# Dilated attention by residue classes instead of masked full steps, with the squares' sums of the attention tail on the tensor engine

## The chip, the cores and the metric

One Trainium2 chip (trn2), all 8 cores. The batch of 16 sequences is split over the cores, two sequences each, and every core runs the same program on its own two, one after the other. The time is the device time of the slowest core in microseconds (us). TensorE is called PE below, VectorE DVE, ScalarE ACT, GpSimd POOL, SyncE SP; PSUM is the memory that PE writes its results to. The form of a matmul is the size of its stationary tile, rows*columns (128*128, 64*128 or 128*64); where two matmuls in a row have different forms, that is a change of form.

Some executions of any kernel here fall into a slower state, in which the cores of one die (or of both) show a lower granted TensorE clock: one such run of the changed kernel had 0.85 to 0.86 on die 1 and 0.99 on die 0, and took 3242.6 us. Such runs are marked slow and are left out of all comparisons.

## The reference

A decoder layer: half a SwiGLU feed-forward network (FFN), a mixer, and another half FFN, each between two RMS norms. The mixer has 4 differential heads and 8 dilated heads of 64 columns. What matters here are the dilated heads:

```python
DIL_PATTERNS = ((128, 1), (512, 4), (2048, 16))   # (window, dilation)

def dilated_pattern(q, k, v, slopes, window, dil):
    """query t attends t, t-d, t-2d, ..., t-window."""
    ...
    bias = -slopes[:, None, None] * (dsub * dil)       # true token distance
    s = jnp.where(valid, s * D ** -0.5 + bias, -inf)
    ...                                                # softmax: o, lse
    return o, lse

def dilated_attention(q, k, v, slopes):
    ...                                                # the three patterns
    w = jax.nn.softmax(jnp.stack(lses, axis=0), axis=0)
    return sum(w[i][..., None] * outs[i] for i in range(3))

def hybrid_mixer(h, ...):
    ...
    return jnp.concatenate([o_d, o_l], axis=-1) @ w_out
```

Weighting the three softmaxes by their own denominators is one softmax in which a key counts once for every pattern that holds it. With count(d) = [d <= 128] + [d % 4 == 0 and d <= 512] + [d % 16 == 0 and d <= 2048], the weight of a key at distance d is count(d) * exp(score - slope * d). Both kernels compute that. At distances from 129 to 512 three keys in four have the count 0, beyond 512 fifteen in sixteen.

## The kernel before

The program is written by a scheduler in the host code: it keeps a model of when each engine will be free, and picks at each point a score step (S), a value step (A) or a piece of other work (F: a projection matmul, a transpose), so that PE has something to do while exponentials and multiplies are under way. Heads are handled in 8 units: units 0 to 3 are one differential head each (with two score maps), units 4 to 7 two dilated heads each. While unit u runs, the projections of unit u+1 are its filler; the last unit's filler is the output projection.

A step of a unit covers 512 queries and 128 keys, for both heads (or maps); `...` marks what is cut here and below:

```python
steps = [(Q, kt) for Q in range(NTT) for kt in range(4 * Q + 4)]       # 40 steps a unit
...
def do_scores(Q, kt, ji):
    mp = kt - 4 * Q
    c0 = max(mp, 0) * 128
    ...
    for m in range(2):                                                 # one head in each 64 rows of PE
        S.op(PE, lambda e, m=m: e.matmul(
            sp[:, m, c0:TT], KT[i][64 * m:64 * m + 64, kt * 128:(kt + 1) * 128],
            QT[i][64 * m:64 * m + 64, Q * TT + c0:(Q + 1) * TT], start=True, stop=True), ...)
    ...
            S.op(ACT, lambda e, ...: e.activation(o_, i_, AF.Exp, bias=bias, scale=SCALE), ...)
    ...
        lazy.append((bm, cost, lambda: S.op(DVE, lambda e: e.tensor_tensor(   # dilated: x count mask (bf16)
            P[:, :, c0:TT], P[:, :, c0:TT],
            masks[:, m0 + c0:m0 + TT].unsqueeze(1).broadcast_to([128, 2, TT - c0]), ALU.mult), ...)))

def do_av(Q, kt, ji):
    for m in range(2):
        for uq in uqs:                                                 # 128 queries each
            S.op(PE, lambda e, ...: e.matmul(
                a_ap, P[:, m, uq * 128:(uq + 1) * 128], Vt[i][:, kt, vc:vc + w1], ...))   # w1 = 65
```

The 65th column of the values is ones, so that the denominator comes out beside the output. The output has queries in the partitions; a reciprocal and a multiply close it, and four transposes on PE bring it into the form that the output projection reads.

The sum of squares for the norm after the output projection is kept by POOL, 512 columns at a time, and PE adds over the partitions once at the end:

```python
class Stat:
    def add(self, si):
        ...
            S.op(POOL, lambda e: e.tensor_tensor(dst[:], sacc[k][:], sq[si][:], ALU.add), ...)
    def finish(self, k2):
        S.op(PE, lambda e: e.matmul(bank(pb), ones_bf[:], ssum[k][:], start=True, stop=True), ...)
        return rstd(pb, k2, ...)
```

The softmax here doesn't subtract the row's maximum and nothing guards it: scores larger than these inputs give would overflow.

Of the kernel before, what the change touches and what calls it, by code (L numbers as in the profile page):

```python
# [23 lines left out]
TT = 512  # L24
# [6 lines left out]
MOFF, MLEN = 384, 1536  # L31
# [197 lines left out]
def _dil_count(d):  # L229
    c = np.zeros_like(d, dtype=np.float32)  # L230
    c += ((d >= 0) & (d <= 128))
    c += ((d >= 0) & (d % 4 == 0) & (d <= 512))
    c += ((d >= 0) & (d % 16 == 0) & (d <= 2048))
    return c


def _consts():
    masks = _dil_count(np.arange(-MOFF, MLEN - MOFF)[None, :] - np.arange(128)[:, None])
# [6 lines left out]
    return masks, tri, btab, ident  # L245


def build_program():
# [10 lines left out]
    masks_d = dt_in("c_masks", [128, MLEN])  # L259
# [3 lines left out]
    outT_d = nc.dram_tensor("outT", [NSEQ, D, SEQ], F32, kind="ExternalOutput").ap()  # L263
    wdb_d = [nc.dram_tensor("wdb%d" % i, [NKC, 128, NF * 128], BF16, kind="Internal").ap() for i in range(2)]

    with ExitStack() as st:
# [5 lines left out]
        U_B = 79936  # L272
# [3 lines left out]
        masks = sb("masks", [128, MLEN], BF16)  # L276
# [6 lines left out]
        lamv = sb("lamv", [128, 256], F32)  # L283
# [7 lines left out]
        sg = [sb("sg%d" % i, [128, TT], F32) for i in range(2)]  # L291
# [25 lines left out]
        QT, KT, Vt, B_QT, B_KT, B_V, B_V1 = [], [], [], [], [], [], []  # L317
# [15 lines left out]
        assert off <= o_y + 16384  # L333
        off = o_y + 16384
        o_tail = off
        o0, B_o0 = [], []
        for i in range(2):
            o = carve(2048)
            o0.append(U[:, o // 2:o // 2 + 1024].bitcast(F32).rearrange("p (a c) -> p a c", a=4))
            B_o0.append([RU.buf("o0_%d_%d" % (i, a), o + a * 512, o + a * 512 + 512) for a in range(4)])  # L340
        NP = 5
# [6 lines left out]
        o = carve(2048)  # L348
        osq = U[:, o // 2:o // 2 + 1024].bitcast(F32).rearrange("p (a c) -> p a c", a=4)
        B_osq = RU.buf("osq", o, o + 2048)  # L350
        Otok, B_Otok = [], []
        for i in range(2):
            o = carve(1024)
            Otok.append(U[:, o // 2:o // 2 + 512].rearrange("p (a c) -> p a c", a=4))
            B_Otok.append([RU.buf("Otok%d_%d" % (i, a), o + a * 256, o + a * 256 + 256) for a in range(4)])
        assert off <= U_B, (off, U_B)
# [26 lines left out]
        def y_mix(d):  # L383
            return xn[:, d, 2 * TT:4 * TT].bitcast(F32), B_yo[d]

        y_free = [U[:, o // 2:o // 2 + TT * 2].bitcast(F32)
                  for o in [NKC * SEQ * 2 + k * 2048 for k in range(6)] + [o_y + 12352]] + [sg[0][:]]
        B_ya = [RU.buf("ya%d" % k, o, o + 2048)
                for k, o in enumerate([NKC * SEQ * 2 + k * 2048 for k in range(6)] + [o_y + 12352])]
        B_sg = [Buf("sg%d" % i) for i in range(2)]  # L390
        B_ya.append(B_sg[0])
# [6 lines left out]
        B_lam = Buf("lam")  # L398
# [4 lines left out]
        B_sml = [[Buf("sml%d_%d" % (i, j)) for j in range(5)] for i in range(3)]  # L403
        B_wdb = [[Buf("wdb%d_%d" % (i, d)) for d in range(NKC)] for i in range(2)]
# [41 lines left out]
        def late_consts():  # L446
# [7 lines left out]
            S.op(DVE, lambda e: e.reduce_sum(lamt[:, 0:1], lamv[:, 0:64], AX.X), reads=[B_lam], writes=[B_lam])  # L454
            S.op(DVE, lambda e: e.reduce_sum(lamt[:, 1:2], lamv[:, 128:192], AX.X), reads=[B_lam], writes=[B_lam])
            S.op(ACT, lambda e: e.activation(lamt[:, 2:4], lamt[:, 0:2], AF.Exp), reads=[B_lam], writes=[B_lam])
            S.op(DVE, lambda e: e.scalar_tensor_tensor(lamt[:, 4:5], lamt[:, 3:4], -LAM_INIT, lamt[:, 2:3],
                                                       ALU.add, ALU.subtract),
                 reads=[B_lam], writes=[B_lam])
            S.dma(POOL, ident[:], ident_d, writes=[B_cpool], kb=32)  # L460
            S.dma(POOL, tri[:], tri_d, writes=[B_cpool], kb=32)
            S.dma(POOL, masks[:], masks_d, writes=[B_cpool], kb=384)
# [6 lines left out]
        class Stat:  # L469
# [19 lines left out]

            def finish(self, k2):  # L490
# [4 lines left out]

        stat_banks = [6, 7]
# [15 lines left out]
        def prenorm_items(tt, gcol, tag):  # L512
            state = {}

            def p_sq(kc):
                def fn():
                    if kc == 0:
                        assert not pre_active
                        pre_active.append(1)
                        state["st"] = Stat(0)  # L520
# [806 lines left out]
```

## Time and profile before

Five runs before the prediction: median 2996.79 us, from 2992.37 to 3129.73 (the longest is a slow run). I cut the attention of each sequence into four stages by what PE does, with one rule for every kernel, so a few borders differ by up to 3 us from those in the prediction. "Steady" begins with the first matmul of a dilated form (in the kernel before that is a 65-column value product, and 8 dilated score matmuls already stand in the 5 us ahead of it) and ends with the first matmul of the output projection; "mixed" ends with the last value or denominator product; "tail" ends where the second FFN begins (16 FFN matmuls that run early in the kernel before, from 1036.7 us, are counted back at the full rate).

| stage, us of the slowest core (before) | sequence 0 | sequence 1 | what PE has in it |
|---|---|---|---|
| differential | 261.8 | 263.0 | differential heads, projections as filler |
| steady | 167.2 | 167.8 | dilated heads, projections as filler |
| mixed | 75.9 | 74.2 | rest of the last dilated unit, output projection as filler |
| tail | 44.2 | 42.7 | rest of the output projection, norms |
| sum | 549.1 | 547.7 | |

How to read it: the change touches the last three rows, 287 us of sequence 0 and 285 of sequence 1. The rest of the 2990.8 us of the profiled core is the differential stage and the FFNs. The cores differ in one place: the tail of sequence 0 lasts about 45 us on cores 1 and 6 (the slowest) and about 35 on the six others, for a reason that I did not look into.

### The profile page before, as it was taken

How to read it: one execution, taken by the hardware profiler on the slowest of the kernel's cores; microseconds unless marked ns; L12 is line 12 of the kernel's file. 1: busy time of each engine (PE TensorE's matmuls, PEld its weight loads, DVE VectorE, ACT ScalarE, POOL GpSimd, SP SyncE). 2: the span in 40 equal slices, each digit the busy share in tenths (PEclk: the TensorE clock that was granted, in tenths of full speed). 3: DMA queues.
4: the chain of work that ended last, by engine and by line, in shares of the span. 5: the costliest groups of instructions: out<-in, count | busy, mean ns of one | idle time of the engine just before them, and what ended most of it. 6: DMA issues, size and time to landing. Idle time of an engine off the chain costs nothing.

```text
span 2990.8 us, 51544 instructions; the slowest of 8 cores (2975.5 to 2990.8 us)
## 1 busy us (share of the span) xinstructions
PE 2808.1 (94%) x17982; PEld 1366.0 (46%) x17982; DVE 1172.0 (39%) x2246; ACT 1368.6 (46%) x2366; POOL 622.9 (21%) x629
## 2 busy tenths in 40 slices
PE   6999998898998699999999999989989978999997
PEld 2444444455554244444444444435555533444443
DVE  2313215554676632132122222255456766322212
ACT  4223324776788632233223233257758884223112
POOL 1212214101002611221222222140110035112002
PEclk9999999999999899999999999999999999999999
DMA  8955433112230153673574444410111103436534
GB/s 186 132 145 119 71 111 80 22 22 42 37 44 12 20 94 72 196 145 72 189 149 76 143 88 81 126 41 12 23 19 23 20 5 63 72 99 162 106 89 144
DMA packets 72139, 250.55 MB, mean 84 GB/s; under 512 B 7376, under 2 KB 7760, under 8 KB 71376
## 3 DMA queue, kind: packets, MB, share of 16 engines
q0 software_dynamic: 35760, 121.06, 25.1%
q1 hardware_dynamic: 36128, 126.18, 12.9%
q8 instruction: 152, 2.49, 0.3%
q14 instruction: 99, 0.81, 0.1%
HBM read 351.49 MB, written 28.31 MB: 127 GB/s over the span
## 4 chain that ended last, share of the span: by engine, by line
PE 85%; DVE 5%; issue 3%; ACT 3%; POOL 2%; DMA 1%; SPq 0%; DVEq 0%; POOLq 0%; ACTq 0%
PE ps L656 41%; PE ps L683 17%; PE ps L786 8%; PE ps L933 7%; PE ps L881 5%; PE ps L802 4%; PE ps L838 2%; POOL sacc L480 1%; ACT U L903 1%; DVE U L572 1%; DVE U L792 1%; POOL sacc L486 1%; DVE xT_sb L563 1%; PE ps L1009 1%; DVE U L919 1%
## 5 line engine op out<-in xcount | busy, mean ns | idle before, releaser
L656 PE MATMUL ps<-xn,W 128*128 128x512 bf16 x3584 | 785.6, 379 | 0.0
L903 ACT ACTIVATE U<-ps,btab 128x256 bf16<-128x256 f32 (+3 forms) x1216 | 692.9, 647 | 177.7 <-PE ps L881 155.9
L665 DVE TENSOR_TENSOR U<-sg,ps 128x512 bf16<-128x512 f32 x352 | 242.0, 688 | 969.2 <-PE ps L656 728.0
L663 ACT ACTIVATE sg<-ps 128x512 f32<-128x512 f32 x352 | 210.2, 597 | 817.6 <-PE ps L656 804.8
L656 PEld LDWEIGHTS ps<-xn,W 128*128 128x128 bf16 x3584 | 350.7, 98 | 422.6
L656 PE MATMUL ps<-xn,U 128*128 128x512 bf16 x2048 | 461.3, 382 | 9.3 <-ACT sq L599 6.3
L683 PE MATMUL ps<-U,W 128*128 128x512 bf16 x2112 | 463.7, 379 | 0.0
L486 POOL TENSOR_TENSOR sacc<-sacc,sq 128x512 f32<-128x512 f32 x230 | 282.4, 1232 | 383.8 <-ACT sq L599 219.1
L683 PEld LDWEIGHTS ps<-U,W 128*128 128x128 bf16 x2112 | 206.6, 98 | 249.2
L656 PEld LDWEIGHTS ps<-xn,U 128*128 128x128 bf16 x2048 | 201.3, 98 | 257.0 <-issue 19.8
L933 PE MATMUL ps<-U 128*128 128x129 bf16 (+1 forms) x4352 | 290.5, 209 | 29.7 <-DVE U L919 20.4
L596 ACT ACTIVATE U<-ps,gains 128x512 f32<-128x512 f32 x158 | 109.0, 690 | 431.0 <-PE ps L683 378.6
L786 PE MATMUL ps<-xn,W 128*128 128x512 bf16 x1024 | 277.0, 385 | 30.5 <-DVE U L792 9.7
L933 PEld LDWEIGHTS ps<-U 128*128 128x128 bf16 x4352 | 223.1, 99 | 145.2 <-issue 112.6
L572 DVE TENSOR_TENSOR U<-U,rst 128x512 f32<-128x512 f32 x158 | 111.2, 711 | 379.6 <-ACT rst L508 379.6
L480 POOL TENSOR_TENSOR sacc<-sq 128x512 f32<-128x512 bf16 x46 | 114.2, 2485 | 661.6 <-ACT sq L599 478.2
L881 PE MATMUL ps<-U 64*128 64x512 bf16 (+3 forms) x1280 | 232.5, 359 | 5.0 <-ACT U L903 4.3
L919 DVE TENSOR_TENSOR U<-U,masks 128x1024 bf16<-128x1024 bf16 (+1 forms) x320 | 192.3, 630 | 34.3 <-ACT U L903 33.1
L683 PE MATMUL ps<-U 128*128 128x512 bf16 x704 | 158.8, 382 | 5.9 <-DMA U<-wdb 5.9
L802 PE MATMUL ps<-W,xn 128*128 128x128 bf16 x2048 | 142.2, 221 | 12.6 <-DVE U L1011 4.4
L533 DVE SCALAR_TENSOR_TENSOR xn<-xT_sb,gains,rst 128x512 bf16<-128x512 f32 x176 | 130.5, 768 | 60.1 <-ACT rst L508 60.1
L838 PE MATMUL ps<-U,W 128*128 128x512 bf16 x512 | 137.9, 412 | 15.6 <-ACT rst L506 7.3
(65 smaller groups left out, 1658.8 us busy)
## 6 DMA issues: line engine op xcount, KB each, us to landing
W<-wdb SPq DMA_DIRECT2D x96, 704.0 KB, 4.4
W<-wgu POOLq DMA_DIRECT2D x112, 512.0 KB, 6.2
U<-wgu POOLq DMA_DIRECT2D x64, 512.0 KB, 6.1
U<-wdb SPq DMA_DIRECT2D x32, 704.0 KB, 4.3
outT<-xT_sb SPq DMA_DIRECT2D x14, 1024.0 KB, 5.4
xT_sb<-xT SPq DMA_DIRECT2D x12, 1024.0 KB, 9.9
W<-win POOLq DMA_DIRECT2D x48, 256.0 KB, 5.1
wdb<-wd POOLq DMA_DIRECT2D x16, 704.0 KB, 16.9
```

Source lines behind the costliest of these rows:

```text
L486: S.op(POOL, lambda e: e.tensor_tensor(dst[:], sacc[k][:], sq[si][:], ALU.add), reads=[B_sacc[k], B_sq[si]], writes=[bd], cost=1.25)
L656: S.op(PE, lambda e, pb=pb, gu=gu, kc=kc, wap=wap, tt=tt: e.matmul(bank(pb), wap[:, (gu * NKC + kc) * 128:(gu * NKC + kc + 1) * 128], xn[: ...
L663: S.op(ACT, lambda e, gi=gi, pg=pg: e.activation(sg[gi][:], bank(pg), AF.Silu), reads=[B_ps[pg]], writes=[B_sg[gi]], cost=c_act(512))
L665: S.op(DVE, lambda e, gi=gi, pu=pu, f=f, tl=tl: e.tensor_tensor(hT[:, f, tl * TT:(tl + 1) * TT], sg[gi][:], bank(pu), ALU.mult), reads=[B_ ...
L683: S.op(PE, lambda e, wap=wap, pb=pb, k=k, tl=tl: e.matmul(bank(pb), wap[:, k * 128:(k + 1) * 128], hT[:, k, tl * TT:(tl + 1) * TT], start= ...
L786: S.op(PE, lambda e, kc=kc: e.matmul(bank(pb), wap[:, kc * 128:(kc + 1) * 128], xn[:, kc, ts(tt)], start=(kc == 0), stop=(kc == NKC - 1)), ...
L802: S.op(PE, lambda e, kc=kc: e.matmul(bank(pb)[:, tq * 128:(tq + 1) * 128], xn[:, kc, t * 128:(t + 1) * 128], wap[:, kc * 128:(kc + 1) * 12 ...
L838: S.op(PE, lambda e, k=k: e.matmul(bank(pb), wap[:, k * 128:(k + 1) * 128], mixT[:, k, ts(tt)], start=(k == 0), stop=(k == NKC - 1)), read ...
L881: S.op(PE, lambda e, m=m: e.matmul(sp[:, m, c0:TT], KT[i][64 * m:64 * m + 64, kt * 128:(kt + 1) * 128], QT[i][64 * m:64 * m + 64, Q * TT + ...
L903: S.op(ACT, lambda e, o_=o_, i_=i_, bias=bias: e.activation(o_, i_, AF.Exp, bias=bias, scale=SCALE), reads=rd + [B_btab], cost=c_act(n), w ...
L919: lazy.append((bm, cost, lambda: S.op(DVE, lambda e: e.tensor_tensor(P[:, :, c0:TT], P[:, :, c0:TT], masks[:, m0 + c0:m0 + TT].unsqueeze(1 ...
L933: S.op(PE, lambda e, a_ap=a_ap, m=m, uq=uq, vc=vc, first=first: e.matmul(a_ap, P[:, m, uq * 128:(uq + 1) * 128], Vt[i][:, kt, vc:vc + w1], ...
```

## The change

The intent: compute fewer scores, and take the end of the attention off POOL.

1. A dilated unit has 18 steps instead of 40. For each 512 queries, two "near" steps hold the distances up to 128, and one step per 512 keys holds the distances divisible by 4: it splits queries and keys by their residue modulo 4 and multiplies only equal residues (four matmuls of 128 keys x 128 queries for a head). Keys are read with a stride of 4; values by residue come from a copy that goes through DRAM.
2. One exponential of 1024 columns a step, without bias, and one multiply by an fp32 table count(d) * exp(-slope * d).
3. Value products are turned round: 64 value columns are stationary and the weights stream, one head in PE columns 0 to 63 and the other in 64 to 127. The output comes out already transposed. Denominators are a product with 64 columns of ones. ACT makes their reciprocals as exp(-ln).
4. Q and K leave PSUM on ACT or DVE, by the scheduler's model.
5. In the tail, PE sums the squares (one 512-column matmul with ones for each square), for four of the norms, 32 matmuls a sequence; the others stay on POOL.
6. Buffers move (tables share memory with the FFN's gate buffer), and weight copies are issued earlier.

The diff, cut to its core:

```diff
+            def dil_items(u):
 ...
+                def segs_of(Q, kind, kb):
+                    if kind < 2:                      # the two near steps
 ...
+                    return [(lambda rows, r=r: KT[i][rows, kb * TT + r:(kb + 1) * TT:4],
+                             lambda m, r=r: V4[i][:, kb, r, 64 * m:64 * m + 64],
 ...
+                             lambda ap, r=r: ap[:, r * 128:(r + 1) * 128], 128) for r in range(4)]
+
+                def sc(Q, kind, kb):
 ...
+                            S.op(PE, lambda e, m=m, rows=rows, kf=kf, col=col, qs=qs: e.matmul(
+                                col(bank(S_pair[si] + m)), kf(rows), qs(QT[i][rows, ts(Q)]), start=True, stop=True,
+                                skip_group_check=True),
 ...
+                    S.op(ACT, lambda e: e.activation(
+                        P[:], bank(S_pair[si], 2).rearrange("p (m q) -> p m q", m=2), AF.Exp, scale=SCALE),
 ...
+                        S.op(DVE, lambda e: e.tensor_tensor(pv, pv, t_, ALU.mult),
+                             reads=flat + [Bt], writes=flat, cost=1.2)
 ...
+                def av(Q, kind, kb, pi):
 ...
+                            S.op(PE, lambda e, m=m, rows=rows, vf=vf, col=col, qs=qs, j=j: e.matmul(
+                                qs(O_[rows, :]), vf(m), col(P[:, m, :]), start=(kind == 0 and j == 0), stop=last,
+                                skip_group_check=True),
 ...
+                            S.op(PE, lambda e, m=m, rows=rows, col=col, qs=qs, j=j: e.matmul(
+                                qs(L_[rows, :]), ones_bf[:, 0:64], col(P[:, m, :]), start=(kind == 0 and j == 0),
 ...
+                def finish(Q):
 ...
+                    S.op(ACT, lambda e: e.activation(rinv[:], L_, AF.Ln), ...)
+                    S.op(ACT, lambda e: e.activation(rinv[:], rinv[:], AF.Exp, scale=-1.0), ...)
+                    S.op(DVE, lambda e: e.tensor_tensor(
+                        mixT[:, u, ts(Q)].rearrange("p (i r) -> p r i", r=4), by_r(O_), by_r(rinv[:]), ALU.mult), ...)
 ...
-                                    S.op(DVE, lambda e: e.tensor_copy(dst[:, ts(tt)], bank(pb)),
+                                    if S.t[ACT] + 0.2 < S.t[DVE]:
+                                        S.op(ACT, lambda e: e.copy(o_, i_), ...)
+                                    else:
+                                        S.op(DVE, lambda e: e.tensor_copy(o_, i_), ...)
 ...
+        class StatPE:
+            def flush(self):
 ...
+                S.op(PE, lambda e: e.matmul(bank(pb), ones_bf[:], sq[si][:], start=(n == 0), stop=(n == NKC - 1)), ...)
 ...
             while fill.peek() is not None or later:
+                if not fill.open:
+                    pe_tail[0] = True
+                    out_banks["y"] = [0, 1, 2, 3]
 ...
-            out_banks["y"] = [0, 1, 2, 3, 4, 5]
-            stat_banks[:] = [6, 7]
+            pe_tail[0] = True
+            out_banks["y"] = [0, 1, 2, 3]
```

## The prediction

> **What bounds the kernel now.** I read the page's busy table first, then the stretches by stage, then the groups by shape, then the timeline of one stage. The page:
>
> ```profile
> PE 2808.1 (94%) x17982; PEld 1366.0 (46%) x17982; DVE 1172.0 (39%) x2246; ACT 1368.6 (46%) x2366; POOL 622.9 (21%) x629
> ...
> PE 85%; DVE 5%; issue 3%; ACT 3%; POOL 2%; DMA 1%; SPq 0%; DVEq 0%; POOLq 0%; ACTq 0%
> ```
>
> PE is the bound on average, so any gain is PE work removed or PE idleness closed. The change touches attention only, so I cut the first sequence's attention into stages (borders: first projection, first 65-column matmul, first output projection, last epilogue, start of the second FFN). The second sequence has the same borders plus 1474 us.
>
> ```profile
> 494.50:757.00 262.50, 231.15 (x2313) 135.89 (x2311) 141.33 (x392) 182.35 (x310) 38.67 (x46) 0.98 0.15 26
> 757.00:923.00 166.00, 159.68 (x1872) 92.38 (x1870) 117.08 (x241) 140.93 (x282) 9.67 (x19) 1.00 0.28 42
> 923.00:1001.00 78.00, 62.67 (x454) 27.00 (x453) 51.69 (x79) 63.35 (x118) 30.63 (x23) 0.87 0.00 1
> 1001.00:1045.40 44.40, 29.97 (x127) 12.44 (x127) 28.63 (x35) 22.49 (x38) 36.95 (x25) 0.92 0.14 25
> ```
>
> Columns: stretch, length, then PE, PEld, DVE, ACT, POOL busy, and granted clock. Differential heads: 262.5 us. Dilated heads before any output projection ("steady"): 166 us, PE busy 96%, ACT 85%, DVE 71%: PE bound, others close. Last dilated unit with output projection ("mixed"): 78 us at clock 0.87. Rest of the output projection ("tail"): 44.4 us with PE busy for 30. The two last are not PE bound; the timeline shows PE released by ACT and POOL:
>
> ```profile
> 1008.77 1.89 PE L838 MATMUL ps<-U,W 128*128 128x512 bf16 x8 [2.08 <-ACT sq L599]
> 1011.89 3.61 PE L838 MATMUL ps<-U,W 128*128 128x512 bf16 x16 [1.23 <-ACT sq L599]
> ...
> 1019.75 0.59 PE L492 MATMUL ps<-ssum,ones_bf 128*128 128x512 bf16 x1 [2.15 <-POOL ssum L486]
> ```
>
> Inside the steady stage the spacing of starts gives real PE costs, since busy counts overlapped latencies:
>
> ```profile
> 855.94 0.61 PE L786 MATMUL ps<-xn,W 128*128 128x512 bf16 x2
> 856.38 0.41 PE L933 MATMUL ps<-U 128*128 128x65 bf16 x8
> 856.72 0.39 PE L881 MATMUL ps<-U 64*128 64x512 bf16 x2
> 857.04 1.07 PE L802 MATMUL ps<-W,xn 128*128 128x128 bf16 x16
> 858.09 0.40 PE L933 MATMUL ps<-U 128*128 128x65 bf16 x8
> ```
>
> Two 512-column projection matmuls take 0.44 us (0.216 each). Two 64-row score matmuls take 0.32 together: they overlap (0.216), plus about 0.1 for entering or leaving the 64-row form. Sixteen 128-column matmuls take 1.05 (0.061 each, taking 32 in 1.95 elsewhere), eight 65-column ones 0.34 (0.031 each, plus a switch). Check on 780 to 900 us (186 score, 634 value, 176 and 354 projection matmuls by the counts of that window): streams 17.2 + 19.7 + 38.0 + 21.6, with 2.4 for transposes, 98.9 us; the other 21.1 us over 186 changes of form is **0.113 us per change**.
>
> **What the Trainium skill says.** "TensorEngine Tiling (Array Packing)", Key Properties: changing the tiling mode drains TensorE; the 0.113 us agrees. The same page's Performance Considerations and "TensorE: Matmul & The Clock Gate", Part 3, say that column-tiled matmuls (64 stationary columns) run side by side as row-tiled ones do. This trace shows it for rows only; the change relies on columns too. "VectorE: DVE Perf Modes", the perf-mode tier table and the errata section: tensor_tensor with fp32 runs at 1x, (N+151)/0.96 ns. The trace agrees: 688 ns for 512 elements with an fp32 input (the L665 row below), while the bf16 mask multiply of 1024 (L919) takes 716, about twice the rate. "ScalarE: Activation LUTs", Table sets: one set holds exp and ln. The trace agrees: table loads stand at L663 and L506, none at the attention's Ln (L988).
>
> **The change, part by part.**
>
> 1. Dilated scores. Before, a unit visits all 40 (query tile, key tile) steps, 34 full ones in area, and multiplies by a count mask. After, 18 steps: per query tile two near steps (distance to 128) and one per 512-key block for distances divisible by 4, sorted by residue. Per sequence 4 units: 160 steps become 72.
>
> 2. Per step, PE after: scores as 4 overlapping pairs, values as 4 column pairs giving the output already transposed, and a denominator pair (64 ones columns x 512). Estimates: 4 x 0.061 = 0.24, 0.24, 0.22. The transposes go. Counting the built instruction streams from first dilated score to first output projection: projections 80, scores 15.7, values 15.0, denominators 14.0, others 0.6: 125.5 us. Before, for its steady stage: 79.3 + 23.3 + 26.7 + 3.4 = 132.7. The reason that the stream falls so little: denominators are new work and projections are fixed.
>
> 3. Changes of form fall from 245 to 176 in that stage: 245 x 0.113 = 27.7 and 176 x 0.113 = 19.9. Before then comes to 160.4, and the stage lasted 166, so 6 us idle. After: 125.5 + 19.9 + 7 idle = 152 us, though it reaches further into the last unit: only 11.3 us of stream are left for "mixed" (46.1 before), with 15 changes: 13, plus about 4 of waiting at the ends of query tiles, 17 us.
>
> 4. ACT and DVE. The groups that the new cost is read from (count, busy us, mean ns of one):
>
> ```profile
> L903 ACT ACTIVATE U<-ps,btab 128x1024 bf16<-128x1024 f32 x168 | 181.3, 1110 | 73.0 <-PE ps L881 68.1 <-DVE U L976 1.2 <-ACT U L903 1.1
> ...
> L665 DVE TENSOR_TENSOR U<-sg,ps 128x512 bf16<-128x512 f32 x352 | 242.0, 688 | 969.2 <-PE ps L656 728.0 <-ACT sg L663 216.6 <-PE ps L492 24.6
> L919 DVE TENSOR_TENSOR U<-U,masks 128x1024 bf16<-128x1024 bf16 x224 | 154.6, 716 | 20.5 <-ACT U L903 19.8
> ```
>
> 72 exponentials of 1110 ns are 80 us per sequence. Added: Ln and Exp of the denominators, 16 x (0.60 + 0.63) = 20 us; some Q/K evacuations move to ACT (0.6 each, some 16 in the stage: 10 us). The multiply has an fp32 table now: (1024+151)/0.96 = 1224 ns, an estimate from that page, 72 x 1.22 = 88 us, against 160 multiplies before (the page's L919 row has 320 with 192.3 us busy), 96 us: fewer but dearer. With some 29 evacuations and 14 closing multiplies of 0.69, DVE has about 115 us of the 152 and ACT about 105, against 117 and 141 of 166 before: neither bounds.
>
> 5. Tail. The squares' sums go from POOL to PE (32 matmuls, 6.9 us), with four output banks. Stream of the tail by the count: 47.9 + 6.9 + 0.4 = 55.2 us. ACT per 128-row block is 0.69 + 0.59 + 0.63 = 1.91 us against PE 8 x 0.216 + 0.22 = 1.95: balanced, so about 11 us of waiting: 66 us. POOL's sums, which also slowed DVE (multiplies of 512 at 1640 instead of 690 ns from 1005 to 1013 us), are out of the way.
>
> 6. Off the path: value copies through DRAM (128 KB out and back a tile, a unit ahead), 768 KB tables, weight copies moved earlier. DMA share is at most 0.28 in these stages.
>
> Sum per sequence: 152 + 17 + 66 = 235 us against 166 + 78 + 44.4 = 288.4. Gain 53, twice 107: **2890 us**. FFNs and differential heads: no change.
>
> **Rivals.** (a) Column pairs don't overlap. Then values and denominators cost double: +32 us a sequence, gain 21, about 2955 us. For: no such matmul in the trace, and each needs its own weight load. Against: the row pairs overlap fully. Half of it (only weight loads serialise) gives 2920. (b) DVE becomes the bound: with 1640 ns instead of 1224 the 72 multiplies cost 118, DVE 145 of 152, and waits appear: 2915. For: exp, multiply and value product form a chain with two score buffers. Against: POOL, with which the 1640 ns values coincide, is nearly idle in the steady stage. (c) The tail doesn't shrink: evacuation and post-norm (0.71 + 0.77 us of DVE a block) bind instead of POOL, tail 80: 2918. (d) More gain: the mixed stage's half-rate clock (matmuls of 512 at 428 ns near 969 us) goes altogether and the tail is dense: 2855.
>
> **Range and chances.** 2890, between (d) and half of (a) or of (a) with (c): 2850 to 2935 should hold 8 in 10. Two per cent is 2937, which needs (a) nearly whole or two rivals at once: faster 0.90, within 2% 0.08, slower 0.02.
>
> **What would show it.** Steps 2 and 3 right: steady stage near 152 us with PE over 93% busy; value pairs spaced 0.06 us, not 0.12; denominator pairs 0.22, not 0.43. Step 4 right: multiplies near 1.22 us, few PE waits for them. Step 5 right: from the last value product to the FFN some 66 us, clock near 1.0, no wait for POOL. Wrong: if differential heads or FFNs move by over 5 us, or if PE in the steady stage waits for DVE.

## The result, and the profile after

A ratio in this document is the mean time of one kernel's fast runs over the mean time of the other's fast runs in the same rounds, so it is not quite the ratio of the medians.

| | median us | runs | range |
|---|---|---|---|
| before | 2998.38 | 16 | 2992.37 to 3338.72 |
| changed | 2875.90 | 9 | 2873.33 to 3242.62 |

Ratio of the fast runs 0.9593, 95% interval 0.9584 to 0.9603: 4.1% faster, 14 us below the predicted 2890, and inside the range. The head of the page of the changed kernel (slowest core 0), busy times and the chain that ended last:

```profile
PE 2736.1 (95%) x17446; PEld 1338.9 (47%) x17446; DVE 1098.4 (38%) x1870; ACT 1228.9 (43%) x1942; POOL 527.9 (18%) x564
...
PE 87%; DVE 5%; issue 3%; ACT 2%; DMA 2%; POOL 1%; SPq 0%; DVEq 0%; POOLq 0%; ACTq 0%
```

PE was and is the bound. Its busy time fell by 72 us and the profiled span by 116 (2990.8 to 2874.6), so the rest is time in which PE no longer stands idle. Where, the stretches of sequence 0 tell (differential, steady, mixed, tail; columns: from:to, length, then busy us and instructions of PE, PEld, DVE, ACT, POOL, granted clock, DMA share, GB/s):

```profile
495.20:756.30 261.10, 229.22 (x2285) 135.90 (x2283) 135.81 (x373) 182.07 (x306) 38.77 (x46) 0.97 0.27 38
756.30:906.20 149.90, 144.64 (x1802) 86.28 (x1800) 107.30 (x112) 97.15 (x128) 9.26 (x15) 0.98 0.31 66
906.20:919.50 13.30, 13.30 (x139) 6.39 (x138) 8.60 (x7) 9.86 (x15) 2.56 (x2) 1.00 0.23 41
919.50:980.50 61.00, 56.40 (x257) 24.34 (x256) 37.42 (x53) 46.93 (x83) 12.96 (x12) 1.00 0.05 9
```

| stage, us | before, seq. 0 / 1 | changed, seq. 0 / 1 | predicted for changed |
|---|---|---|---|
| differential | 261.8 / 263.0 | 261.1 / 263.9 | no change |
| steady | 167.2 / 167.8 | 149.9 / 149.9 | 152 |
| mixed | 75.9 / 74.2 | 13.3 / 13.3 | 17 |
| tail | 44.2 / 42.7 | 61.0 / 61.0 | 66 |
| the last three | 287.3 / 284.7 | 224.2 / 224.2 | 235 |

Read mixed and tail together, for the border between them depends on how much output projection is done before the last unit ends: 120.1 us became 74.3. That is 46 of the 63 us that sequence 0 gained on these two cores; the steady stage gave 17. In the new mixed stage PE is busy all 13.3 us at clock 1.00; before it was busy for 62.67 of 78 us at 0.87.

PE in the steady stage, starts and lengths:

```profile
791.77 0.41 PE L1066 MATMUL ps<-U 64*128 64x128 bf16 x8
792.12 0.41 PE L1098 MATMUL ps<-U 128*64 128x128 bf16 x8
792.37 0.38 PE L1107 MATMUL ps<-U,ones_bf 128*64 128x512 bf16 x2
792.68 0.61 PE L815 MATMUL ps<-xn,W 128*128 128x512 bf16 x2
```

"128*64" is the stationary tile: 128 rows, 64 columns. From start to start: 8 score matmuls of 128 columns take 0.35 us (4 pairs of 0.061 and a change of form), 8 value matmuls 0.25 (4 x 0.061, so the two heads run side by side), two denominator matmuls of 512 columns 0.31 (one stream of 0.216 and a change of form).

The groups of the new step, by shape (count, busy us, mean ns of one, idle time before and its releaser):

```profile
L1073 ACT ACTIVATE U<-ps 128x1024 bf16<-128x1024 f32 x144 | 141.8, 1020 | 75.4 <-PE ps L1066 74.7 <-DVE U L1085 0.4
L1085 DVE TENSOR_TENSOR U<-U,SG 128x1024 bf16<-128x1024 bf16 x72 | 85.6, 1245 | 2.1 <-ACT U L1073 2.1
...
L1125 DVE TENSOR_TENSOR U<-ps,U 128x512 bf16<-128x512 f32 x32 | 41.8, 1307 | 79.0 <-ACT U L1123 44.3 <-PE ps L1066 34.8
```

The exponential takes 1020 ns, not 1110. The Trainium skill, "ScalarE: Activation LUTs", section "What ACT_TABLE_LOAD costs", gives an activation 186 ns + 0.833 ns a column with immediate scale and bias, and about 93 ns more for each per-partition pointer operand: for 1024 columns 1039 and 1132 ns. The trace agrees within 2%: 1020 without the bias table, and 1110 with it (the L903 row in the prediction). The multiplies take 1245 ns (1236 with the other table buffer), as estimated. The last row is the multiply that closes a query tile; it takes 1307 ns, and I had counted 690.

What PE waits for, first in mixed and tail of the kernel before (core 6, 923 to 1046 us; releaser: us in total, times, longest), and then in the tail of the changed kernel (919 to 981 us):

```profile
PE ps L492 <- POOL ssum L486: 7.5, 3, 5.0
PE ps L933 <- DVE U L919: 7.2, 6, 3.4
PE ps L838 <- ACT rst L506: 4.4, 2, 2.8
```

```profile
PE ps L524 <- ACT sq L563: 3.5, 8, 0.6
PE ps L508 <- POOL ssum L499: 1.1, 1, 1.1
```

POOL's sums and what hung on them are gone from PE's waits but for 1.1 us. The tail on PE, each block of 8 output matmuls followed by one sum:

```profile
931.10 1.89 PE L875 MATMUL ps<-U,W 128*128 128x512 bf16 x8
932.83 0.38 PE L524 MATMUL ps<-sq,ones_bf 128*128 128x512 bf16 x1
933.04 1.46 PE L875 MATMUL ps<-U,W 128*128 128x512 bf16 x6
934.92 0.38 PE L524 MATMUL ps<-sq,ones_bf 128*128 128x512 bf16 x1 [0.42 <-ACT sq L563]
```

Here 8 matmuls and a sum take 1.94 us with no gap; the wait in brackets is the kind that is left.

The stages sum to 63.8 us less for sequence 0 and 59.6 for sequence 1, 123 us, and the profiled spans differ by 116. On the profiled cores the other 7 lie in the FFNs between the two attentions: PE waited 11.1 us for weights there in the changed kernel and 5.9 before. The other cores settle that this is no effect of the change: this wait lies between 5.5 and 11.2 us in both kernels, and the mean length of the stretch between the attentions is 928.1 us before and 928.0 changed. Over the eight cores the three stages fell from 280.9 and 285.1 us to 223.6 and 224.2, 118 us in all, and the mean span by 117 (2984.8 to 2867.4). So 118 is the better figure for what the change brings on a core.

### The profile page after: what moved, and what is told of

Read it like the earlier page. It is cut to its first block, busy times and chain, and to the rows that moved or that the text cites. A ratio compares the mean times of both kernels' runs of the same rounds, so it can differ in the third digit from the quotient of the medians.

```text
span 2874.6 us, 48271 instructions; the slowest of 8 cores (2859.6 to 2874.6 us)
## 1 busy us (share of the span) xinstructions
PE 2736.1 (95%) x17446; PEld 1338.9 (47%) x17446; DVE 1098.4 (38%) x1870; ACT 1228.9 (43%) x1942; POOL 527.9 (18%) x564
## 4 chain that ended last, share of the span: by engine, by line
PE 87%; DVE 5%; issue 3%; ACT 2%; DMA 2%; POOL 1%; SPq 0%; DVEq 0%; POOLq 0%; ACTq 0%
PE ps L697 42%; PE ps L724 18%; PE ps L815 7%; PE ps L945 5%; PE ps L839 4%; PE ps L913 3%; PE ps L875 3%; PE ps L1066 2%; PE ps L1098 2%; PE ps L1107 1%; DVE U L613 1%; DMA U<-wdb 1%; DVE U L973 1%; DMA xT_sb<-xT 1%; DVE U L994 1%
## 5 line engine op out<-in xcount | busy, mean ns | idle before, releaser
L706 DVE TENSOR_TENSOR U<-SG,ps 128x512 bf16<-128x512 f32 x352 | 241.9, 688 | 939.6 <-PE ps L697 718.9
L704 ACT ACTIVATE SG<-ps 128x512 f32<-128x512 f32 x352 | 210.0, 597 | 811.2 <-PE ps L697 802.1
L697 PEld LDWEIGHTS ps<-xn,W 128*128 128x128 bf16 x3584 | 350.6, 98 | 422.8
L724 PE MATMUL ps<-U,W 128*128 128x512 bf16 x2112 | 463.7, 379 | 0.0
L926 ACT ACTIVATE U<-ps,btab 128x256 bf16<-128x256 f32 (+3 forms) x512 | 335.1, 717 | 125.9 <-PE ps L913 113.1
L499 POOL TENSOR_TENSOR sacc<-sacc,sq 128x512 f32<-128x512 f32 x190 | 223.9, 1179 | 367.5 <-ACT sq L640 200.6
L945 PE MATMUL ps<-U 128*128 128x129 bf16 x2176 | 176.3, 224 | 11.4 <-DVE U L932 6.3
L1073 ACT ACTIVATE U<-ps 128x1024 bf16<-128x1024 f32 x144 | 141.8, 1020 | 75.4 <-PE ps L1066 74.7
L724 PE MATMUL ps<-U 128*128 128x512 bf16 x704 | 160.3, 384 | 11.1 <-DMA U<-wdb 11.1
L945 PEld LDWEIGHTS ps<-U 128*128 128x128 bf16 x2176 | 130.4, 99 | 69.6 <-issue 60.8
L815 PEld LDWEIGHTS ps<-xn,W 128*128 128x128 bf16 x1024 | 87.9, 99 | 132.2 <-issue 62.6
L839 PEld LDWEIGHTS ps<-W,xn 128*128 128x128 bf16 x2048 | 119.4, 99 | 26.8 <-issue 21.8
```

Source lines behind the costliest of these rows:

```text
L697: S.op(PE, lambda e, pb=pb, gu=gu, kc=kc, wap=wap, tt=tt: e.matmul(bank(pb), wap[:, (gu * NKC + kc) * 128:(gu * NKC + kc + 1) * 128], xn[: ...
L704: S.op(ACT, lambda e, gi=gi, pg=pg: e.activation(sg[gi], bank(pg), AF.Silu), reads=[B_ps[pg]], writes=[B_sg[gi]], cost=c_act(512))
L706: S.op(DVE, lambda e, gi=gi, pu=pu, f=f, tl=tl: e.tensor_tensor(hT[:, f, tl * TT:(tl + 1) * TT], sg[gi], bank(pu), ALU.mult), reads=[B_sg[ ...
L724: S.op(PE, lambda e, wap=wap, pb=pb, k=k, tl=tl: e.matmul(bank(pb), wap[:, k * 128:(k + 1) * 128], hT[:, k, tl * TT:(tl + 1) * TT], start= ...
L815: S.op(PE, lambda e, kc=kc: e.matmul(bank(pb), wap[:, kc * 128:(kc + 1) * 128], xn[:, kc, ts(tt)], start=(kc == 0), stop=(kc == NKC - 1)), ...
L839: S.op(PE, lambda e, kc=kc: e.matmul(bank(pb)[:, tq * 128:(tq + 1) * 128], xn[:, kc, t * 128:(t + 1) * 128], wap[:, kc * 128:(kc + 1) * 12 ...
```

## The experiments

The theory after the result: PE's stream in the steady stage shrank because the two heads share PE in columns and changes of form became fewer, and mixed and tail shrank because the last unit is short and PE's own sums replaced POOL's; ACT and DVE have slack. Rivals: the column sharing is worth little (then the fewer steps alone would have done it); DVE is the real bound of the steady stage; the new tail alone, without the new algorithm, would have brought the gain; the scheduler's interleaving costs more than the arithmetic. Differences below are of ratios to the kernel before in the same rounds, times 2997 us; with the intervals of the two ratios such a difference is good to 5 to 7 us (17 for tail_pool). The runs that shared a chip with a second run of the changed kernel (after_again) are compared with that directly.

**Same columns (same_cols).** Both heads of a block step write the same 64 output partitions, so they share the PE columns and can't overlap. The numbers are wrong (relative error 0.143).

```diff
+                    orow = (lambda r_: slice(0, 64)) if kind == 2 else (lambda r_: r_)
-                                qs(O_[rows, :]), vf(m), col(P[:, m, :]), ...
+                                qs(O_[orow(rows), :]), vf(m), col(P[:, m, :]), ...
-                                qs(L_[rows, :]), ones_bf[:, 0:64], col(P[:, m, :]), ...
+                                qs(L_[orow(rows), :]), ones_bf[:, 0:64], col(P[:, m, :]), ...
```

> The changed kernel, but in the steps by 512-key block both heads' value and denominator matmuls write the same 64 output rows (wrong result on purpose), so that a pair shares its column tile. Theory (column pairs overlap, and PE sets the time): value and denominator streams of these steps double, 10 x (0.245 + 0.216) = 4.6 us a unit, 8 units: +37 us, about 2913. Rival (pairs gain nothing by lying in different columns): no change, 2876.

Measured: fast runs 2904.19 to 2907.56, ratio 0.9705, 34 us over the changed kernel's 0.9593. Steady 164.8 us instead of 149.9, mixed 15.4 instead of 13.3, tail the same 61.0. PE's timeline (core 5), value and denominator products of a block step:

```profile
802.10 0.63 PE L1099 MATMUL ps<-U 128*64 128x128 bf16 x8
802.57 0.59 PE L1108 MATMUL ps<-U,ones_bf 128*64 128x512 bf16 x2
803.10 1.07 PE L839 MATMUL ps<-W,xn 128*128 128x128 bf16 x16
```

The 8 value matmuls take 0.47 us from start to start instead of 0.25, the two denominator matmuls 0.53 instead of 0.31: each doubles its stream. 0.44 us for each of 40 block steps a sequence is 17.6 us, 35 for both; 34 were measured. Column sharing is real, and its loss shows in full in the time.

**Full array (full_array).** The other way of losing the sharing: 128 stationary columns instead of 64 in the block steps, in the ordinary form (wrong, relative error 0.103).

```diff
-                             lambda m, r=r: V4[i][:, kb, r, 64 * m:64 * m + 64],
+                             lambda m, r=r: V4[i][:, kb, r, 0:128],
+                    orow = (lambda r_: slice(0, 128)) if kind == 2 else (lambda r_: r_)
-                                qs(L_[rows, :]), ones_bf[:, 0:64], col(P[:, m, :]), ...
+                                qs(L_[orow(rows), :]), ones_bf[:, 0:(128 if kind == 2 else 64)], col(P[:, m, :]), ...
```

> The changed kernel, but in the steps by 512-key block each head's value and denominator matmul uses all 128 stationary columns (wrong result on purpose), so these run one after the other in the form of the projections. Theory: stream +37 us as with a shared column tile, but 22 fewer changes of form per sequence (-5 us): about 2908. Rival (changes of form matter more than column pairs): below 2876.

Measured: fast runs 2901.00 to 2902.84, ratio 0.9673, 24 us over the changed kernel. The timeline (core 6):

```profile
802.39 0.61 PE L1099 MATMUL ps<-U 128*128 128x128 bf16 x8
802.84 0.59 PE L1108 MATMUL ps<-U,ones_bf 128*128 128x512 bf16 x2
803.27 1.06 PE L839 MATMUL ps<-W,xn 128*128 128x128 bf16 x16
```

The streams double as with same columns (0.45 for the values, 0.43 for the denominators, which is 2 x 0.216), but the step from the denominators to the next projection costs nothing, since both have the full form: 0.43 against 0.53 in same_cols. That gap of 0.10 us is one change of form, seen by itself. By the streams full_array has 22 changes fewer a sequence than the changed kernel (169 instead of 191 in steady and mixed stage), some 5 us in all; the two runs differ by 10. The longer streams, 0.20 and 0.12 us for each of 40 block steps a sequence, make 26 us; 24 were measured.

**Without the denominators (no_denoms).** The denominator products of the block steps are left out (wrong, relative error 0.159).

```diff
-                    for j, (_, _, _, _, col, qs, n) in enumerate(parts):
+                    for j, (_, _, _, _, col, qs, n) in enumerate(parts if kind < 2 else []):
```

> The changed kernel without the denominator matmuls of the steps by 512-key block (wrong result on purpose). Theory (the PE stream sets the time): 80 pairs of 0.216 us are gone, -17 us over both sequences, with 11 more changes of form a sequence, +2.5: about 2861. Rival (another engine or chain bounds): 2876.

Measured: fast runs 2864.44 to 2868.03, ratio 0.9552: 12 us less. Steady 145.5 and 147.2 us, mixed 11.8. Their bare stream is 80 x 0.216 = 17 us, and the scheduler, which then places other work between, built 13 more changes of form in the steady stage (189 instead of 176), 1.5 us a sequence. So the denominators cost 12 us in all, and the new work was not free.

**Multiply table in bf16 (bf16_table).** The table is loaded as bf16, to shorten the multiply; its load moves from the SP to the POOL queue. Correct within the tolerance.

```diff
-        tbl = [SG[:], U[:, o_tail // 2:o_tail // 2 + 3072].bitcast(F32)]
+        tbl = [SG[:, 0:TBL].bitcast(BF16), U[:, o_tail // 2:o_tail // 2 + 2 * TBL]]
-                S.dma(SP, tbl[u % 2], tbl_d[u - 4], writes=[B_tbl[u % 2]], kb=768)
+                S.dma(POOL, tbl[u % 2], tbl_d[u - 4], writes=[B_tbl[u % 2]], kb=768)
```

> The changed kernel with its weight tables in bf16 instead of fp32, same instruction order. The multiply should fall from 1.24 to about 0.70 us, 37 us of VectorE per sequence. Theory (PE bounds, VectorE has slack): 2868 to 2878, no clear change. Rival (the chain exp, multiply, value product bounds): 2830 to 2850.

Measured: 2875.08 and 2874.08 in the fast runs (three more were slow), ratio 0.9600: no change. The steady stage and the multiply group of this kernel (core 2):

```profile
755.70:905.40 149.70, 143.48 (x1802) 85.89 (x1800) 74.20 (x113) 97.25 (x128) 10.31 (x18) 0.99 0.30 57
```

```profile
L1085 DVE TENSOR_TENSOR U<-U,SG 128x1024 bf16<-128x1024 bf16 x72 | 48.3, 714 | 16.7 <-ACT U L1073 16.7
```

The multiply fell from 1245 to 714 ns, DVE's busy time in the stage from 107 to 74 us, and the stage stayed at 149.7. In the changed kernel as it stands, DVE's work is hidden: PE waits 1.2 us a sequence for the multiply there, and here not at all. On this core PE waits 2.0 us (4.8 in sequence 1, whose stage takes 152.7) for the copy of the values through DRAM instead; over the cores the stage is 148.6 and 149.6 us in the mean, against 149.1 and 149.7, so nothing large is covered up by that.

**All evacuations on DVE (evac_dve).** Q and K leave PSUM on DVE always, as before the change.

```diff
-                                    if S.t[ACT] + 0.2 < S.t[DVE]:
+                                    if False:
```

> The changed kernel with all query and key evacuations back on VectorE (72 of 128 were on ScalarE): +25 us of VectorE per sequence in about 411 us of attention before the output projection. Theory (PE bounds there): within 0.3% of 2876. Rival (VectorE is close to its limit in the dilated units): 2890 or more.

Measured: fast runs 2893.28 to 2899.62, ratio 0.9652, 18 us slower: the theory that both engines have ample slack failed, and the rival held. The steady stage (core 6), and what PE waits for in it (756 to 918 us):

```profile
756.20:918.20 162.00, 150.08 (x1819) 87.46 (x1818) 124.32 (x141) 81.95 (x98) 9.24 (x15) 0.97 0.29 61
```

```profile
PE ps L1098 <- DVE U L1085: 6.5, 12, 1.9
```

DVE is busy 124 us of 162, only 77%, and yet PE waits 12 times for the multiply. Against the changed kernel 29 more DVE instructions lie in the stage (141 against 112), 17 us of work, and the stage grew by 12 us. An average share does not show this; the chain score, exponential, multiply, value product has only two score buffers, and a DVE that comes late is late for PE too. PE's listed waits account for half of the 12 us (11.6 us instead of 5.3); the other half stands in its busy time (150.1 instead of 144.6 us), and I can't say why.

**Both together (evac_dve_bf16).** All evacuations on DVE, and the bf16 table: if DVE's load was the cause, the loss must go.

> All query and key evacuations on VectorE (which alone cost about 18 us) and bf16 weight tables (which alone changed nothing), instruction order as with fp32 tables. Theory (VectorE is near its limit in the dilated units: the 1.24 us multiplies delay evacuations and value products; the evacuations on ScalarE bought the slack): the multiply at 0.7 us gives the slack back, 2876 to 2882, and the stage of the dilated units returns from 162 to about 150 us. Rival (the evacuation's place itself or the changed order costs it): stays at 2890 to 2896.

Measured: fast runs 2873.38 to 2878.75, mean 2876.0 against 2875.2 of the changed kernel on the same chip. The loss is gone; the steady stage is back at 152.6 and 150.8 us, and PE's waits for the multiply in it (core 0, 756 to 908 us) fell to 1.5 us:

```profile
PE ps L1098 <- DVE U L1085: 1.5, 2, 1.3
```

So the cause was DVE's load. The choice of engine for the evacuations, which I had entered as 10 us of ACT work, is part of what makes the change pay: with the fp32 table it is worth 18 us.

**The changed kernel once more (after_again).** Run on the same chip as the last group, to have a base there.

> The changed kernel itself, as reference for the other runs of this call on the same chip: ratio 0.959 to the kernel before, about 2876 us, by every theory.

Measured: fast runs 2874.61 to 2875.75, ratio 0.9577 (interval 0.9545 to 0.9609). The result repeats.

**Sums back on POOL (tail_pool).** The new algorithm with the old tail.

```diff
-                if not fill.open:
-                    pe_tail[0] = True
-                    out_banks["y"] = [0, 1, 2, 3]
-            pe_tail[0] = True
-            out_banks["y"] = [0, 1, 2, 3]
+            out_banks["y"] = [0, 1, 2, 3, 4, 5]
+            stat_banks[:] = [6, 7]
```

> The changed kernel with the sums of squares of the output projection back on POOL, everything else as changed. Theory (the sums on PE shorten the tail): the stretch from the last value product to the second FFN grows from 61 us to about 76 to 80 per sequence, because 48 POOL additions of 1.2 to 1.6 us fill it and slow the VectorE; 2876 becomes about 2905. Rival (the tail is bound by ScalarE evacuation, and only the short last unit made it dense): without the 32 sum matmuls per sequence (6.9 us) it is the same or shorter, 2862 to 2876.

Measured: three of five runs were slow. The two others took 2916.06 and 2938.86, ratio 0.9777 with an interval of 0.9721 to 0.9832, which the 2% rule calls unclear. In the longer one, which was profiled, cores 0 and 1 are somewhat disturbed (clock 0.970 and 0.972, spans 2937 and 2925); in the shorter one all cores lie between 2909 and 2915. I take the shorter, a single run: 40 us more than the changed kernel. The tail of sequence 0 on an undisturbed core (core 3), and PE's waits in it:

```profile
916.80:998.40 81.60, 57.91 (x229) 23.30 (x228) 47.84 (x54) 47.62 (x83) 56.95 (x41) 0.85 0.05 8
```

```profile
PE ps L875 <- ACT sq L640: 14.1, 3, 7.6
PE ps L508 <- POOL ssum L499: 4.8, 2, 3.7
```

The tail takes 81.6 us instead of 61.0 (81.6 in sequence 1 too), with POOL busy for 57 of them. PE waits for POOL directly, and through ACT: ACT's own longest wait in this stretch is for POOL's sums (8.8 us), which free its squares' buffers. The clock of 0.85 stands in both sequences of this undisturbed core, so it belongs to this tail. The steady stage of 149.8 and mixed of 13.3 are as in the changed kernel. So the new algorithm alone brings the three stages from 287.3 to 244.7 us, and the sums on PE bring them to 224.2: twice 20.5 us, which is the 40 measured. The rival "the tail doesn't shrink", with a tail of 80, would have been right without part 5 of the change.

**The old algorithm with the new tail (before_defer).** The kernel before, with the sums on PE in the tail; for them to engage, the output projection must not start before the last unit has ended, so it is held back.

```diff
+        class StatPE:
 ...
-                    while out_next < NTT - 1 and (7, out_next) in mix_done:
+                    while False:
 ...
+                if not fill.open:
+                    pe_tail[0] = True
+                    out_banks["y"] = [0, 1, 2, 3]
```

> The kernel before, with only the tail part of the change, and the output projection started after the last unit as it nearly does in the changed kernel. Theory (the old last unit is what spoils the overlap, the dense tail costs 61 us): last unit alone some 48 us by ScalarE plus 61 = 109 against 120.5 now: -23 us, about 2975. Rival (the tail part brings the whole gain of 46 us a sequence by itself): 2905. Second rival (without filling work the old unit waits): 2998 or slower.

Measured: fast runs 2982.01 to 2985.51, ratio 0.9948 (interval 0.9930 to 0.9967): 16 us better than before, where 23 were expected. So the new tail alone does not bring the gain; but the run also holds the output projection back, and the two are not separated. The three stages of sequence 0 are 278.0 us (287.3 on the slowest core before, 224.2 changed). Its last unit, which now has no filler for PE, and the tail behind it (core 1):

```profile
912.00:962.10 50.10, 43.38 (x438) 23.70 (x436) 32.36 (x67) 45.13 (x86) 1.58 (x3) 0.71 0.12 17
962.10:1035.50 73.40, 67.09 (x301) 29.04 (x302) 38.04 (x57) 49.90 (x88) 7.13 (x8) 0.97 0.05 8
```

This is what the mixed stage hid: one old unit by itself takes 50 us, with ACT busy for 45 of them. It is bound by ACT, and PE meanwhile gets a clock of 0.71. The new unit has 18 exponentials of 1020 ns and 8 activations of about 0.6 us for the reciprocals, 23 us of ACT. From the last projection matmul to the last value product it is 45 us here (917.3 to 962.1) and 15 us in the changed kernel (904.5 to 919.5), which does 34 matmuls of the output projection in that time besides. So of the 54 us between 278.0 and 224.2, 30 lie in the last unit, in which ACT was the bound and not PE.

**Two score steps at a time (group_scores).** If changes of form cost 0.113 us each, grouping score steps in twos should save some. The scheduler issues a second score step right after the first, and holds the first until both buffers are free.

```diff
+                if r_s < inf and len(todo) > 1 and (avq or fill.peek() is not None):
+                    both = B_S[0] + B_S[1]
+                    if len(avq) <= NP - 3:
+                        r_s = max(r_s, S.ready(rd, both))
+                    elif len(avq) > 1:
+                        r_s = inf
 ...
                 if pick == "S":
                     todo.popleft()
                     fn()
+                    if todo and len(avq) < NP - 1:
+                        tag, rd, wr, fn = todo[0]
+                        if (tag is None or tag in ptags) and S.ready(rd, wr()) <= S.t[PE] + 0.1:
+                            todo.popleft()
+                            fn()
```

> The changed kernel with score steps issued two at a time, when both score buffers are free. Changes of matmul form before the output projection fall from 483 to 335 per sequence by the built instruction streams. Theory (each change costs 0.113 us of PE and PE bounds): -148 x 0.113 x 2 = -33 us, about 2843. Rival (holding a score step back leaves ScalarE and then PE waiting): 2876 or slower.

Measured: 2928.33 and 2930.30 us in the two runs that count as fast, 53 us over the changed kernel. Part of that is not the kernel's: in each of the two runs two cores are disturbed (clock 0.975 to 0.978) and set the time, while the six others lie between 2889 and 2904, 25 us or so over the changed kernel's. On one of these (core 0) the attention of the two sequences takes 500.1 and 500.3 us instead of 485.3 and 488.1, together 27 us more. So the loss is about 25 us, and the theory failed. Differential and steady stage (core 7, one of the disturbed ones; its steady stage is as on the others, and its differential stage is among the shortest, 275.9 to 282.3 us on the eight cores), and PE's longest waits in the first of them:

```profile
494.70:771.40 276.70, 232.26 (x2381) 138.83 (x2379) 137.88 (x375) 181.24 (x310) 37.96 (x46) 0.98 0.26 38
771.40:914.90 143.50, 134.20 (x1716) 79.90 (x1716) 111.69 (x119) 90.12 (x115) 9.24 (x15) 0.98 0.34 65
```

```profile
PE ps L815 <- DVE U L829: 6.2, 8, 2.5
PE ps L945 <- DVE U L973: 4.1, 15, 0.4
```

Changes of form in the differential and steady stages fell from 483 to 335, worth 17 us a sequence, but the differential stage grew by 15.6 us (18 in the mean of the cores). 32 projection matmuls of 512 columns and 64 of 128 moved into it from the steady stage, 10.8 us of stream. That is more than the 6.4 us by which the steady stage shrank, so no stage got faster for its work. In the differential stage PE waits for DVE, which comes late while both score buffers fill and drain together. Fewer changes were paid for with a broken pipeline.

**Grouping in the dilated units only (group_dil), and with the bf16 table (group_dil_bf16).** The same edit under the condition u_next > 4; the second also takes the bf16 table and tells the scheduler 0.72 us for the multiply instead of 1.2.

```diff
-                if r_s < inf and len(todo) > 1 and (avq or fill.peek() is not None):
+                if u_next > 4 and r_s < inf and len(todo) > 1 and (avq or fill.peek() is not None):
```

> Score steps issued two at a time in the dilated units only. Changes of form fall by 26 per sequence by the built streams. Theory: 26 x 0.113 x 2 = 6 us less, 2868 to 2872; the 6.4 us that the stage lost in the first grouped run is partly work that had moved into the differential stage. Rival (the grouped order costs waits here too): 2876 or more.

> Two score steps at a time in the dilated units, bf16 tables, and the order built for a 0.72 us multiply. Changes of form fall by 52 per sequence: 52 x 0.113 x 2 = 12 us less, about 2864, if PE sets the time; a candidate for the best version. Rival: shorter multiplies and fewer changes are eaten by waits, 2872 or more.

Measured on the chip of after_again (mean 2875.2): group_dil 2881.0 in the mean, 6 us slower, although changes in the steady stage fell from 176 to 152. Its steady stage is 153.2 us, and PE waits there (756 to 910 us, core 7) above all for the multiply:

```profile
PE ps L1098 <- DVE U L1085: 5.0, 8, 1.2
```

group_dil_bf16: five fast runs of 2866.63 to 2868.95, mean 2867.7, correct. Changes fall to 130 in the steady stage, which lasts 146.4 and 147.3 us, and no wait for the multiply appears in the list of PE's waits of that stage in sequence 0. It is 0.3% faster than the changed kernel, all runs below all of its fast runs on that chip, and has a ratio of 0.9552 to the kernel before. Taking 52 changes away (46 in the steady stage, 6 in the mixed) at 0.113 us makes 5.9 us a sequence, 12 in all; 7.5 were measured, 0.07 us a change. This is the best version found: each of its parts by itself brought nothing or a loss, and together they pay. The waits say why: PE waits 5.0 us in this stage for the multiply when the grouping stands alone, and 0.5 us in the whole run with the bf16 table. The run changes the order of the steps too (52 changes fewer instead of 26), and no run separates that.

## Why the prediction was right, and where its sizes were off

- **Steps 1 to 3 (steps, streams, changes of form).** Right. The steady stage lasts 149.9 us, predicted 152. The changed kernel has 176 changes, as counted, and PE waits about 5 us (3.2 for the transposes of the last differential unit, 1.2 for a multiply, 0.9 for an evacuation) instead of 7. That the heads overlap in columns was the step most in doubt; same_cols shows it and its worth, 34 us. The 0.113 us a change is a little high: it takes the whole rest of the window of 120 us, in which PE stood idle for 1.75 us (busy 118.25); without these it is 0.104, and the gap between same_cols and full_array is 0.10.
- **Mixed stage.** "13, plus about 4 of waiting at the ends of query tiles": the stream was right (13.3), and the 4 us of waiting didn't come: the list of PE's waits between 906 and 920 us is empty. Output projection is there to fill every end of a query tile.
- **Step 5 (tail).** "about 11 us of waiting": mis-sized. The stream was counted as 55.2 us, and the stage took 61.0, so 5.8 us beyond it; PE's listed waits are 4.6. Balanced engines with four banks lose less than I allowed. That POOL's sums had to go is shown by tail_pool.
- **The sum.** 235 predicted, 224.2 found: 2.1 from the steady stage, 3.7 from mixed, 5.0 from the tail. On the other side I had used 288.4 for both sequences before, and they were 287.3 and 284.7. So these stages gave 123.6 us in all on the profiled cores where I predicted 107, and 118 in the mean of the cores. That the number came so close is in part luck: I put the stages 22 us too long after the change, and took the time before from the slowest core, 11 us above the mean of the cores; half of the first error is covered by the second. The sign "FFNs move by over 5 us" seems to be met on the profiled cores (7 us), and is not in the mean (928.1 and 928.0).
- **Step 4 (ACT and DVE).** Exponentials were taken over at 1110 ns from a row with a bias table; they are 1020. The closing multiply was taken as 0.69 us and is 1.31; it writes every fourth bf16 element, and a multiply with the same kinds of operands that writes densely takes 688 ns (L706), but no run changes the step alone. Both errors were off the path. The new Ln and Exp take 596 and 631 ns, as counted, and no table load stands at them. "Neither bounds" is true of the kernel as it is (bf16_table: no change) but was too sure: evac_dve shows that 17 us more of DVE work in a stage make it 12 us longer, and cost 18 us in all.
- **Rival (a), no column overlap.** Refuted by the spacing of 0.25 and 0.31 us and by same_cols.
- **Rival (b), DVE the bound.** Not in this kernel, but near. What protects it is the scheduler's sharing of the evacuations.
- **Rival (c), tail 80 us.** Refuted by 61.0; without the sums on PE it would have come true (81.6).
- **Rival (d), 2855.** Part of it came: the half-rate clock of the mixed stage went altogether (1.00), but the tail is not fully dense and the steady stage keeps 176 changes of form.

Not foreseen: that the last unit's gain is a gain on ACT. I read "mixed" as PE idle for want of ACT and POOL, but gave its shrinking to the PE stream alone; before_defer shows ACT busy 90% of an old unit without filler.

## What to carry to other kernels

When a stage has a mean share of 70 to 80% on a second engine, test the slack by giving that engine a little more, not by the share: here DVE was busy for 72% of a stage of 150 us, and 17 us more made the stage 12 us longer. Look at a unit that has no filler, such as the last one of a loop: here it showed a bound (ACT, 90% busy) that the filler had hidden. Matmuls with 64 stationary columns on two heads shared the array at full rate here, but each change of form cost 0.07 to 0.11 us, so count forms as well as columns, and group them only where the engines behind have slack.

## What the Trainium skill lacked or had wrong

- "TensorEngine Tiling (Array Packing)", Key Properties, says that a change of tiling mode drains TensorE and gives no size. The runs: 0.113 us a change from the count over 120 us of the kernel before (0.104 without PE's idle time), and 0.10 us by itself between same_cols (0.53 us) and full_array (0.43 us).
- The same page has "Up to 2×" in theory for tiles of 64, and "TensorE: Matmul & The Clock Gate", Part 3, measured speedups of tiles of 32; for two tiles of 64 columns with a stationary operand each they have no measured figure. Here 8 matmuls of 128 columns take 0.25 us in two columns and 0.47 in one, and two of 512 take 0.31 and 0.53, a change of form included: full overlap.
- "TensorE: Matmul & The Clock Gate", Part 1, says to budget a clock of 13/16 once three cores of a die run dense matmuls. All eight cores run dense here, and fast runs have a granted clock of 0.99 with 0.216 us for 512 columns; a core's mean clock comes near the stated one in slow runs only (0.81 on one die of group_scores, 0.85 to 0.86 on one die of the changed kernel).
- "VectorE: DVE Perf Modes", table of modes, has one element a cycle for 1x for everything, which makes about 690 ns of 512 elements (an estimate with the formula of its errata section). The closing multiply, which writes bf16 elements at a step of 4, took 1307 ns for 512 (1304 to 1309 in all runs), and one with the same kinds of operands and a dense output 688 (L706); that the step is the cause is argued, not tested.
